# Quarter-wise token blocks and parallel accumulator banks in the prologue of an eight-core hybrid encoder layer

## The chip, the cores and the metric

The kernel runs on one Trainium2 chip, on all 8 of its cores. Each core takes one element of the batch and does the same work as the others. The time is the device time of the slowest core in one execution, in microseconds (us).

In the runs here an execution falls into one of two states. In the slow one, the cores of one die (cores 0 to 3 or 4 to 7) show a lower granted clock of TensorE (undisturbed cores have about 0.99), and the time is longer. Only fast executions are compared here. Where the profiled execution of a kernel was slow on one die, only the cores of the other die are read.

## The reference, cut to what matters

One layer projects the input `x` (2048 prompt tokens and 64 sample tokens per core, 2048 channels) onto the inputs of three branches, and merges the branches. The part that matters here is the first branch, a causal attention with 12 heads of 128 channels, whose logits get a bias from cumulated forget logits:

```python
z = einsum('btd,dn->btn', x, w_in)
q, k, v, f, g_fox, ... = split(z)
logf = log_sigmoid(f + fox_bf)                  # one number per token and head
...
cum = transpose(cumsum(logf, axis=1))           # (B, H, S)
s = einsum('bqhd,bkhd->bhqk', q, k) * scale
s = s + cum[..., queries, None] - cum[..., None, keys]
p = softmax(where(causal, s, NEG_INF))
o = einsum('bhqk,bkhd->bqhd', p, v)             # later multiplied by silu(g_fox)
```

Every head needs four projections of `x`: K, Q, V and the gate G, with 128 weight columns each. The forget logits F of all 12 heads are one projection with only 12 columns.

## The kernel before

The 2112 tokens of a core are cut into five blocks x0 to x4, of 424 or 420 tokens. A projection of one block is 16 matmuls, one for each chunk of 128 channels, which add up in one accumulator bank. The prologue makes the projections of head 0. After it, the attention of head 0 starts, with the projections of head 1 mixed in, so that TensorE always has work. Three more names are needed: *cqb* is the cumulated forget logits of a block of queries, written to DRAM and read back to all partitions. *ncc* is the negative of the same numbers for the keys, laid out by transposes on TensorE. The value transposes (`vtrans`) turn V into the layout that attention needs.

All `x` blocks and weights are loaded through one queue that GpSimd fills, in this order. `load_next(0)` to `load_next(3)` bring the weights of K, Q, V and G of head 0, `load_next(4)` those of K of head 1:

```python
load_x(0, 0)                 # first quarter of x0: 4 of 16 chunks
load_next(0)                 # K weights, 0.5 MB
load_x(0, 1)
load_x(0, 2)
load_x(0, 3)
S.add(POOL, DMA(wf[:], I["w_f"]), writes=[r_wf], dmasem=d_wf)     # F weights
load_next(1)                 # Q weights
load_next(2)                 # V weights
load_x(1)                    # whole block, 1.7 MB
load_next(3)                 # G weights
load_x(2)
load_x(3)
load_x(4)
load_cache(0)
for i in range(4, NSLOT):
    load_next(i)
```

The projections run one after another, each to its end:

```python
for tb in range(5):
    if tb == 0:
        runall(g_k(0, 0)); runall(g_f(0))       # printed on two lines in the kernel
    else:
        runall(g_f(tb)); runall(g_k(0, tb))
    runall(g_q(0, tb))
    runall(g_v(0, tb))
    if tb < 3:
        runall(g_g(0, tb))
    if tb == 3:
        for _ in range(2):
            next_cqb()
ncc_group()                  # 25 transposes
for g in range(5):
    runall(vtrans(0, g))     # 17 transposes
next_cqb()
```

In the profile, every matmul and weight load of a projection has the line L148. The tiles tell them apart: `xT_15` to `xT_19` are x0 to x4, `wf` holds the F weights, `ring_20` K, `ring_21` Q, `ring_22` V and `ring_23` G of head 0, and `ring_24` K of head 1. A second number after a name is a buffer number.

The softmax here doesn't subtract the row's maximum and nothing guards it: scores larger than these inputs give would overflow.

Of the kernel before, what the change touches and what calls it, by code (L numbers as in the profile page):

```python
# [8 lines left out]
F32 = mybir.dt.float32  # L9
# [146 lines left out]
def DMA(out, in_, **kw):  # L156
    return lambda e: e.dma_start(out=out, in_=in_, **kw)  # L157
# [29 lines left out]
NS = 64  # L187
# [165 lines left out]
def build():  # L353
# [35 lines left out]
    sconvT = C0.tile("sconvT", [128, 12, 2], F32, [r_c2])  # L389
    r_ncc = Res("ncc")  # L390
    ncc = C0.tile("ncc", [128, 25, H], F32, [r_ncc])
    r_ut = Res("utail")
# [5 lines left out]
    for b, (t0, n) in enumerate(TB):  # L398
        rs = [Res(f"xT{b}_{i}") for i in range(4)]
        xT.append(SB.at(off, f"xT{b}", [128, 16, n], BF16, rs))  # L400
        r_xT.append(rs)
        d_xT.append([S.dmasem(f"xT{b}_{i}") for i in range(4)] if b == 0 else [S.dmasem(f"xT{b}")] * 4)
        off += 32 * n
# [129 lines left out]

    def g_k(h, tb):
        i = h % 2
        def drain(bk, rb, t0, n):
            t, r = kv32.next()
            S.add(ACT, COPY(t[:, 0:n], bk[:, 0:n]), reads=[rb], writes=[r])
            def f():
                S.add(SP, DMA(O["kT_o"][h, :, t0:t0 + n], t[:, 0:n]), reads=[r], dmasem=d_kv[id(r)])  # L540
                S.add(POOL, COPY(kT[i][:, t0:t0 + n], t[:, 0:n]), reads=[r], writes=[r_k[i][tb]])
            E.later(0.7, f)
        return proj(("K", h), tb, drain, tb == 4)

    def g_v(h, tb):
        def drain(bk, rb, t0, n):
# [5 lines left out]
            E.later(0.7, f)  # L552
        return proj(("V", h), tb, drain, tb == 4)

    def g_q(h, tb):
        i = h % 2
        def drain(bk, rb, t0, n):
            S.add(ACT, COPY(qT[i][:, t0:t0 + n], bk[:, 0:n]), reads=[rb], writes=[r_q[i][tb]])
        return proj(("Q", h), tb, drain, tb == 4)

    def g_g(h, tb):
        def drain(bk, rb, t0, n):
            silu(bk, rb, n, sg[tb][:, 0:n], r_sg[tb], True)
        return proj(("G", h), tb, drain, tb == 4)

# [39 lines left out]

    def load_x(b, q=None):
        if q is None:
            S.add(POOL, DMA(xT[b][:], I[f"xT{b}"]), writes=r_xT[b], dmasem=d_xT[b][0])
        else:
            S.add(POOL, DMA(xT[b][:, 4 * q:4 * q + 4, :], I[f"xT{b}"][:, 4 * q:4 * q + 4, :]),  # L610
                  writes=[r_xT[b][q]], dmasem=d_xT[b][q])
    load_x(0, 0)
    load_next(0)
    load_x(0, 1)
    load_x(0, 2)
    load_x(0, 3)
    S.add(POOL, DMA(wf[:], I["w_f"]), writes=[r_wf], dmasem=d_wf)
    load_next(1)
    load_next(2)
    load_x(1)  # L620
    load_next(3)
    load_x(2)
    load_x(3)
    load_x(4)
    load_cache(0)
    for i in range(4, NSLOT):
        load_next(i)
# [15 lines left out]

    def g_f(tb):
        t0, n = TB[tb]
        bk, rb = PJ.next()
        for k in range(16):
            yield E.pe(MM(bk[0:H, 0:n], wf[:, k, :], xT[tb][:, k, 0:n], k == 0, k == 15), n, [r_wf, r_xT[tb][k // 4]], [rb])
        t, r = et.next()
# [12 lines left out]

    def ncc_group():
        bk, rb = PJ.next()
        for c in range(16):
            E.pe(TR(bk[:, c * H:(c + 1) * H], cumP[:, c * 128:(c + 1) * 128], identf[0:H, 0:H]), 96, [r_cum, r_const], [rb])
        for c in range(9):
            n = 128 if c < 8 else NS
            E.pe(TR(bk[0:n, (16 + c) * H:(17 + c) * H], cumS[:, c * 128:c * 128 + n], identf[0:H, 0:H]), 96, [r_cus, r_const], [rb])
        S.add(DVE, TS(ncc[:, 0:24, :], bk[:, 0:24 * H].rearrange("p (a b) -> p a b", b=H), -1.0, ALU.mult),  # L670
              reads=[rb], writes=[r_ncc])
        S.add(DVE, TS(ncc[0:NS, 24, :], bk[0:NS, 24 * H:25 * H], -1.0, ALU.mult), reads=[rb], writes=[r_ncc])

# [83 lines left out]
    def step(s):  # L757
# [16 lines left out]
        if kc == "A":  # L774
            kcT, rk, _, vc, rv, _ = cache[i]
            y, ry = rl.next()
            def pre():
                S.add(DVE, TT(y[:, :].rearrange("p (c q) -> p c q", q=NS),
                              cq[:, 0:NS].unsqueeze(1).broadcast_to([128, 8, NS]),
                              ncc[:, 16:24, h].unsqueeze(2).broadcast_to([128, 8, NS]), ALU.add),  # L780
                      reads=[rcq, r_ncc], writes=[ry])
            pre()
# [23 lines left out]
        S.add(DVE, STT(x[0:kn, n0:n], sb[0:kn, n0:n], SCALE, cq[0:kn, n0:n], ALU.mult, ALU.add), reads=[rs, rcq], writes=[rx])  # L806
        E.later(T_EXP, lambda: S.add(ACT, ACTF(p[0:kn, n0:n], x[0:kn, n0:n], AF.Exp, bias=bias), reads=[rx, r_ncc], writes=[rp]))
        def facc():
# [84 lines left out]

    for tb in range(5):
        if tb == 0:
            runall(g_k(0, 0))
            runall(g_f(0))
        else:
            runall(g_f(tb))
            runall(g_k(0, tb))  # L900
        runall(g_q(0, tb))
        runall(g_v(0, tb))
        if tb < 3:
            runall(g_g(0, tb))
        if tb == 3:
            for _ in range(2):
                next_cqb()
    ncc_group()
    for g in range(5):
        runall(vtrans(0, g))  # L910
    next_cqb()


# [457 lines left out]
```

## Time and profile before

| before | |
|---|---|
| time, first three executions | median 3448.35 us (3447.11 to 3532.04) |
| TensorE busy, on the profile's page | 97% of the span |
| chain of waits that ended last | 93% TensorE |
| start of block 1, mean of cores 0 to 3 | 48.63 us |
| start of attention (load of its first weights), the same cores | 104.41 us |
| 1600th weight load of the core, counted from 0 (inside head 0's attention) | 309.08 us |

The last rows come from the trace. All kernels here load the same 18,761 sets of weights into TensorE on each core, so the n-th load marks about the same point of the work in each of them. The 1600th lies well past the prologue and everything that moved across its end.

The profiled execution of the kernel before had one die in the slow state. This is the view by cores (span and mean granted clock):

```profile
die 0 (median of its cores): 3439.7 us, clock 0.990
die 1 (median of its cores): 3610.0 us, clock 0.936
```

The second die shows clock 0.936 and is left aside. All readings below are of cores 0 to 3, core 0 if not said otherwise.

The page of the profile is that of the slowest core, here one of the slow die, so only its shares are read. It gives the busy time of each engine, and the first line of the chain that ended last:

```profile
PE 3502.0 (97%) x18761; PEld 1845.2 (51%) x18761; DVE 1202.3 (33%) x2092; ACT 1021.2 (28%) x1846; POOL 771.3 (21%) x962
...
PE 93%; DMA 3%; SPq 1%; ACT 1%; issue 1%; DVE 1%; POOL 1%; POOLq 0%; DVEq 0%; ACTq 0%
```

The kernel is bound by TensorE nearly everywhere. A change of the prologue can only win time in which TensorE stands still or runs at half rate there. The timeline of TensorE on core 0 shows where that is. Its columns are start, duration, engine, line, operation, what is written and read, shape, count, and in brackets the idle time before the group and what ended it:

```profile
13.03 1.57 PE L148 MATMUL bank<-xT_15_57,ring_20_62 128*128 128x424 bf16 x4 [13.03 <-DMA ring_20_62<-w_in]
...
43.45 5.60 PE L148 MATMUL bank<-xT_15_57,ring_23_65 128*128 128x424 bf16 x16 [10.56 <-DMA ring_23_65<-w_in]
48.98 3.03 PE L148 MATMUL bank<-xT_16_58,wf_104 128*12 128x424 bf16 x16
51.95 3.04 PE L148 MATMUL bank<-xT_16_58,ring_20_62 128*128 128x424 bf16 x16
54.82 3.03 PE L148 MATMUL bank<-xT_16_58,ring_21_63 128*128 128x424 bf16 x16
...
101.29 1.15 PE L151 MATMUL bank<-identf_44,cumP_107 12*128 12x12 f32 x16
...
102.90 0.62 PE L154 MATMUL bank<-identb_43,vT_73 128*128 128x128 bf16 x8
103.95 0.89 PE L154 MATMUL bank<-identb_43,vT_73 128*128 128x128 bf16 x9 [0.43 <-DVE ncc_54 L179]
```

The reader is to see four things. The first matmul waits 13 us for the first weights. TensorE then stands 10.56 us until the weights of G land. G itself takes 5.60 us, where a projection takes 3.03 otherwise. From there to the end of block 4 no wait appears at all (the lines left out are all of the kind of those shown, without a bracket). At the end stand the ncc transposes (L151), then the value transposes (L154), with one wait of 0.43 us.

The slow G fits the granted clock in the trace: full from 24.8 us, half from 35.1 to 48.7 us, then full for 949 us. TensorE had stood since 32.9 us, so the clock fell 2.2 us into the wait, and it came back 5.3 us after G's first matmul. On these four cores the half-clock stretch is 10.2 or 13.7 us long, and G's matmuls start 0.35 us apart in place of 0.18. What sets the length of the stretch is not shown.

### The profile page before, as it was taken

How to read it: one execution, taken by the hardware profiler on the slowest of the kernel's cores; microseconds unless marked ns; L12 is line 12 of the kernel's file. 1: busy time of each engine (PE TensorE's matmuls, PEld its weight loads, DVE VectorE, ACT ScalarE, POOL GpSimd, SP SyncE). 2: the span in 40 equal slices, each digit the busy share in tenths (PEclk: the TensorE clock that was granted, in tenths of full speed). 3: DMA queues.
4: the chain of work that ended last, by engine and by line, in shares of the span. 5: the costliest groups of instructions: out<-in, count | busy, mean ns of one | idle time of the engine just before them, and what ended most of it. 6: DMA issues, size and time to landing. Idle time of an engine off the chain costs nothing.

```text
span 3614.3 us, 54781 instructions; the slowest of 8 cores (3434.6 to 3614.3 us)
## 1 busy us (share of the span) xinstructions
PE 3502.0 (97%) x18761; PEld 1845.2 (51%) x18761; DVE 1202.3 (33%) x2092; ACT 1021.2 (28%) x1846; POOL 771.3 (21%) x962
## 2 busy tenths in 40 slices
PE   6999999999999989999999999999999999999898
PEld 3444444544444545555555554555555555555343
DVE  1455555555556722222222221111111111111365
ACT  1455555555555410010104552111111111111111
POOL 1222222222222211111111221000022223332133
PEclk8888888888888999999999999999999999999999
DMA  9423333333222243333323216333455545655743
GB/s 167 97 64 70 70 70 68 66 67 66 66 63 66 46 69 65 68 62 56 61 50 59 47 38 164 90 98 85 116 143 133 138 118 131 141 125 136 206 173 117
DMA packets 183608, 337.45 MB, mean 93 GB/s; under 512 B 31204, under 2 KB 135388, under 8 KB 177000
## 3 DMA queue, kind: packets, MB, share of 16 engines
q0 software_dynamic: 39744, 134.55, 22.9%
q1 hardware_dynamic: 143592, 199.39, 17.9%
q8 instruction: 156, 2.56, 0.3%
q14 instruction: 116, 0.95, 0.1%
HBM read 362.26 MB, written 106.13 MB: 130 GB/s over the span
## 4 chain that ended last, share of the span: by engine, by line
PE 93%; DMA 3%; SPq 1%; ACT 1%; issue 1%; DVE 1%; POOL 1%; POOLq 0%; DVEq 0%; ACTq 0%
PE bank L148 93%; DMA ring_23_65<-w_in 1%; SPq L157 1%; DMA a_scr_3<-ao_59_101 1%; PE bank L154 0%; DMA memT_134<-memT 0%; DMA mb_scr<-gt_114_156 0%; DMA x_147_189<-xp 0%; DMA a_4_112_154<-a_scr_4 0%; ACT rl_83_125 L165 0%; DVE on_85_127 L175 0%; ACT pt_71_113 L165 0%; POOL ao_59_101 L175 0%; DVE acc_78_120 L175 0%; ACT qT_74 L170 0%
## 5 line engine op out<-in xcount | busy, mean ns | idle before, releaser
L175 DVE TENSOR_TENSOR mt_115_157<-bank,gt_113_155 128x424 f32<-128x424 f32 (+1 forms) x120 | 71.8, 598 | 517.8 <-PE bank L148 448.5
L175 DVE TENSOR_TENSOR mt_116_158<-bank,gt_114_156 128x424 f32<-128x424 f32 (+1 forms) x120 | 71.8, 598 | 494.1 <-PE bank L148 463.9
L165 ACT ACTIVATE gt_113_155<-bank,bm_50 128x424 f32<-128x424 f32 (+1 forms) x120 | 73.6, 613 | 506.3 <-PE bank L148 455.6
L165 ACT ACTIVATE gt_114_156<-bank,bm_50 128x424 f32<-128x424 f32 (+1 forms) x120 | 73.6, 613 | 499.4 <-PE bank L148 470.8
L148 PE MATMUL bank<-xT_15_57,ring_20_62 128*128 128x424 bf16 x400 | 84.5, 359 | 17.9 <-DMA ring_20_62<-w_in 13.9
L148 PE MATMUL bank<-qT_70,kT_71 128*128 128x512 bf16 (+4 forms) x246 | 96.2, 391 | 0.0
L148 PE MATMUL bank<-qT_74,kT_75 128*128 128x512 bf16 (+4 forms) x246 | 94.5, 384 | 0.2 <-DVE st_69_111 L183 0.2
L148 PE MATMUL bank<-xT_17_59,ring_26_68 128*128 128x424 bf16 x416 | 86.2, 352 | 4.8 <-ACT qT_74 L170 4.8
L148 PE MATMUL bank<-xT_17_59,ring_22_64 128*128 128x424 bf16 x416 | 86.8, 354 | 4.0 <-ACT qT_70 L170 4.0
L148 PE MATMUL bank<-xT_16_58,ring_24_66 128*128 128x424 bf16 x432 | 90.2, 353 | 0.0
L148 PE MATMUL bank<-xT_19_61,ring_24_66 128*128 128x420 bf16 x432 | 89.4, 351 | 0.0
L148 PE MATMUL bank<-xT_15_57,ring_24_66 128*128 128x424 bf16 x432 | 89.2, 356 | 0.0
L148 PE MATMUL bank<-xT_17_59,ring_24_66 128*128 128x424 bf16 x432 | 88.7, 353 | 0.0
L148 PE MATMUL bank<-xT_18_60,ring_24_66 128*128 128x420 bf16 x432 | 88.2, 351 | 0.0
L148 PE MATMUL bank<-xT_16_58,ring_26_68 128*128 128x424 bf16 x416 | 87.7, 354 | 0.0
L148 PE MATMUL bank<-xT_16_58,ring_22_64 128*128 128x424 bf16 x416 | 87.2, 354 | 0.0
L148 PE MATMUL bank<-xT_15_57,ring_26_68 128*128 128x424 bf16 x416 | 86.6, 354 | 0.0
L148 PE MATMUL bank<-xT_15_57,ring_22_64 128*128 128x424 bf16 x416 | 86.2, 354 | 0.0
L148 PE MATMUL bank<-xT_19_61,ring_22_64 128*128 128x420 bf16 x416 | 84.9, 351 | 0.3
L148 PE MATMUL bank<-xT_18_60,ring_22_64 128*128 128x420 bf16 x416 | 85.1, 351 | 0.0
L148 PE MATMUL bank<-xT_19_61,ring_26_68 128*128 128x420 bf16 x416 | 84.5, 349 | 0.4 <-ACT qT_74 L170 0.2
L148 PE MATMUL bank<-xT_18_60,ring_26_68 128*128 128x420 bf16 x416 | 84.5, 349 | 0.0
(917 smaller groups left out, 7352.2 us busy)
## 6 DMA issues: line engine op xcount, KB each, us to landing
ring_24_66<-w_in POOLq DMA_DIRECT2D x15, 512.0 KB, 6.7
ring_21_63<-w_in POOLq DMA_DIRECT2D x14, 512.0 KB, 8.0
ring_22_64<-w_in POOLq DMA_DIRECT2D x14, 512.0 KB, 7.8
ring_23_65<-w_in POOLq DMA_DIRECT2D x14, 512.0 KB, 6.8
ring_25_67<-w_in POOLq DMA_DIRECT2D x14, 512.0 KB, 8.2
ring_26_68<-w_in POOLq DMA_DIRECT2D x14, 512.0 KB, 6.7
ring_27_69<-w_in POOLq DMA_DIRECT2D x14, 512.0 KB, 6.6
ring_20_62<-w_in POOLq DMA_DIRECT2D x13, 512.0 KB, 7.1
```

Of the source, the lines that this page charges most:

```text
L148: return lambda e: e.matmul(out, lhsT=lhsT, rhs=rhs, start=start, stop=stop)
L157: return lambda e: e.dma_start(out=out, in_=in_, **kw)
L165: return lambda e: e.activation(out=out, in_=in_, func=func, **kw)
L175: return lambda e: e.tensor_tensor(out=out, in0=in0, in1=in1, op=op)
```

## The change

The change is meant to make TensorE wait less for data in the prologue. Each of x1 to x4 is loaded in four quarters of 4 chunks, as x0 was. The projections of a block, F, K, V, Q and G, are run quarter by quarter, each in an accumulator bank of its own. So all matmuls that a quarter allows can run before the next quarter lands. Besides that, four things move: the G weights are now loaded before x1; the F weights come after the V weights; block 0 computes F after V; and the first 8 ncc transposes and 12 of the 17 value transposes are put between blocks 3 and 4, while the other ncc transposes run 5 us into attention.

The diff, cut to its core:

```diff
-        d_xT.append([S.dmasem(f"xT{b}_{i}") for i in range(4)] if b == 0 else [S.dmasem(f"xT{b}")] * 4)
+        d_xT.append([S.dmasem(f"xT{b}_{i}") for i in range(4)])
...
-    S.add(POOL, DMA(wf[:], I["w_f"]), writes=[r_wf], dmasem=d_wf)
     load_next(1)
     load_next(2)
-    load_x(1)
+    S.add(POOL, DMA(wf[:], I["w_f"]), writes=[r_wf], dmasem=d_wf)
     load_next(3)
-    load_x(2)
-    load_x(3)
-    load_x(4)
+    for b in range(1, 5):
+        load_x(b)                     # now four quarters each
+    load_next(4)
     load_cache(0)
-    for i in range(4, NSLOT):
+    for i in range(5, NSLOT):
         load_next(i)
...
+    PPJ = Ring(BK)
+    def pro_block(tb, gens):
+        t0, n = TB[tb]
+        bs = [PPJ.next() for _ in gens]
+        for q in range(4):
+            for (key, drain), (bk, rb) in zip(gens, bs):
+                for k in range(4 * q, 4 * q + 4):
+                    ...               # one matmul of this projection, chunk k
+                if q == 3:
+                    ...
+                    drain(bk, rb, t0, n)
...
-    for tb in range(5):
-        ...                           # F, K, Q, V, G one after another
-    ncc_group()
-    for g in range(5):
+    runall(g_k(0, 0))
+    runall(g_q(0, 0))
+    runall(g_v(0, 0))
+    pro_block(0, [(None, d_f(0))])
+    runall(g_g(0, 0))
+    for tb in range(1, 5):
+        gens = [(None, d_f(tb)), (("K", 0), g_k(0, tb, True)), (("V", 0), g_v(0, tb, True)), (("Q", 0), g_q(0, tb, True))]
         if tb < 3:
-            runall(g_g(0, tb))
+            gens.append((("G", 0), g_g(0, tb, True)))
+        pro_block(tb, gens)
         if tb == 3:
-            for _ in range(2):
-                next_cqb()
+            next_cqb()
+            next_cqb()
+            ncc_group(0)
+            for g in range(3):
+                runall(vtrans(0, g))
+    for g in range(3, 5):
         runall(vtrans(0, g))
     next_cqb()
+    E.later(5.0, lambda: ncc_group(1))
```

More of the change, by code (lines that the diff above doesn't have):

```diff
@@ L389, in build @@
     sconvT = C0.tile("sconvT", [128, 12, 2], F32, [r_c2])
-    r_ncc = Res("ncc")
-    ncc = C0.tile("ncc", [128, 25, H], F32, [r_ncc])
+    r_ncc, r_ncc2 = Res("ncc"), Res("ncc2")
+    ncc = C0.tile("ncc", [128, 25, H], F32, [r_ncc, r_ncc2])
     r_ut = Res("utail")
@@ L531, in silu, with g_k @@
         E.later(0.9, s1)
-    def g_k(h, tb):
+    def g_k(h, tb, raw=False):
         i = h % 2
@@ L542, in drain, with g_v @@
             E.later(0.7, f)
-        return proj(("K", h), tb, drain, tb == 4)
-    def g_v(h, tb):
+        return drain if raw else proj(("K", h), tb, drain, tb == 4)
+    def g_v(h, tb, raw=False):
         def drain(bk, rb, t0, n):
@@ L552, in drain, with g_q @@
             E.later(0.7, f)
-        return proj(("V", h), tb, drain, tb == 4)
-    def g_q(h, tb):
+        return drain if raw else proj(("V", h), tb, drain, tb == 4)
+    def g_q(h, tb, raw=False):
         i = h % 2
@@ L558, in drain, with g_g @@
             S.add(ACT, COPY(qT[i][:, t0:t0 + n], bk[:, 0:n]), reads=[rb], writes=[r_q[i][tb]])
-        return proj(("Q", h), tb, drain, tb == 4)
-    def g_g(h, tb):
+        return drain if raw else proj(("Q", h), tb, drain, tb == 4)
+    def g_g(h, tb, raw=False):
         def drain(bk, rb, t0, n):
             silu(bk, rb, n, sg[tb][:, 0:n], r_sg[tb], True)
-        return proj(("G", h), tb, drain, tb == 4)
+        return drain if raw else proj(("G", h), tb, drain, tb == 4)
     def blks(t0, n):
@@ L604, in build, with load_x @@
     et = Ring(ctr.items)
-    def load_x(b, q=None):
-        if q is None:
-            S.add(POOL, DMA(xT[b][:], I[f"xT{b}"]), writes=r_xT[b], dmasem=d_xT[b][0])
-        else:
+    def load_x(b):
+        for q in range(4):
             S.add(POOL, DMA(xT[b][:, 4 * q:4 * q + 4, :], I[f"xT{b}"][:, 4 * q:4 * q + 4, :]),
                   writes=[r_xT[b][q]], dmasem=d_xT[b][q])
-    load_x(0, 0)
-    load_next(0)
-    load_x(0, 1)
-    load_x(0, 2)
-    load_x(0, 3)
-    S.add(POOL, DMA(wf[:], I["w_f"]), writes=[r_wf], dmasem=d_wf)
+    for q in range(4):
+        S.add(POOL, DMA(xT[0][:, 4 * q:4 * q + 4, :], I["xT0"][:, 4 * q:4 * q + 4, :]), writes=[r_xT[0][q]], dmasem=d_xT[0][q])
+        if q == 0:
+            load_next(0)
     load_next(1)
     load_next(2)
-    load_x(1)
+    S.add(POOL, DMA(wf[:], I["w_f"]), writes=[r_wf], dmasem=d_wf)
     load_next(3)
-    load_x(2)
-    load_x(3)
-    load_x(4)
+    for b in range(1, 5):
+        load_x(b)
+    load_next(4)
     load_cache(0)
-    for i in range(4, NSLOT):
+    for i in range(5, NSLOT):
         load_next(i)
@@ L642, in build, with d_f, drain_f @@
     d_cs = [S.dmasem(f"cs{b}") for b in range(6)]
-    def g_f(tb):
+    PPJ = Ring(BK)
+    def pro_block(tb, gens):
         t0, n = TB[tb]
-        bk, rb = PJ.next()
-        for k in range(16):
-            yield E.pe(MM(bk[0:H, 0:n], wf[:, k, :], xT[tb][:, k, 0:n], k == 0, k == 15), n, [r_wf, r_xT[tb][k // 4]], [rb])
+        bs = [PPJ.next() for _ in gens]
+        for q in range(4):
+            for (key, drain), (bk, rb) in zip(gens, bs):
+                for k in range(4 * q, 4 * q + 4):
+                    if key is None:
+                        E.pe(MM(bk[0:H, 0:n], wf[:, k, :], xT[tb][:, k, 0:n], k == 0, k == 15), n, [r_wf, r_xT[tb][q]], [rb])
+                    else:
+                        w, rw = W(key)
+                        E.pe(MM(bk[:, 0:n], w[:, k, :], xT[tb][:, k, 0:n], k == 0, k == 15), n, [rw, r_xT[tb][q]], [rb])
+                if q == 3:
+                    if key is not None and tb == 4:
+                        Wfree(key)
+                    drain(bk, rb, t0, n)
+    def d_f(tb):
+        return lambda bk, rb, t0, n: drain_f(tb, bk, rb, t0, n)
+    def drain_f(tb, bk, rb, t0, n):
         t, r = et.next()
@@ L661, in g_f, with ncc_group @@
             S.add(SP, DMA(cum_scr[:, NP:NP + NS], cumS[:, PAST:PAST + NS]), reads=[r_cus], writes=[r_cscr[5]], dmasem=d_cs[5])
-    def ncc_group():
+    def ncc_group(part):
         bk, rb = PJ.next()
-        for c in range(16):
+        if part == 0:
+            for c in range(8):
+                E.pe(TR(bk[:, c * H:(c + 1) * H], cumP[:, c * 128:(c + 1) * 128], identf[0:H, 0:H]), 96, [r_cum, r_const], [rb])
+            S.add(DVE, TS(ncc[:, 0:8, :], bk[:, 0:8 * H].rearrange("p (a b) -> p a b", b=H), -1.0, ALU.mult),
+                  reads=[rb], writes=[r_ncc])
+            return
+        for c in range(8, 16):
             E.pe(TR(bk[:, c * H:(c + 1) * H], cumP[:, c * 128:(c + 1) * 128], identf[0:H, 0:H]), 96, [r_cum, r_const], [rb])
@@ L669, in ncc_group @@
             E.pe(TR(bk[0:n, (16 + c) * H:(17 + c) * H], cumS[:, c * 128:c * 128 + n], identf[0:H, 0:H]), 96, [r_cus, r_const], [rb])
-        S.add(DVE, TS(ncc[:, 0:24, :], bk[:, 0:24 * H].rearrange("p (a b) -> p a b", b=H), -1.0, ALU.mult),
-              reads=[rb], writes=[r_ncc])
-        S.add(DVE, TS(ncc[0:NS, 24, :], bk[0:NS, 24 * H:25 * H], -1.0, ALU.mult), reads=[rb], writes=[r_ncc])
+        S.add(DVE, TS(ncc[:, 8:24, :], bk[:, 8 * H:24 * H].rearrange("p (a b) -> p a b", b=H), -1.0, ALU.mult),
+              reads=[rb], writes=[r_ncc2])
+        S.add(DVE, TS(ncc[0:NS, 24, :], bk[0:NS, 24 * H:25 * H], -1.0, ALU.mult), reads=[rb], writes=[r_ncc2])
     SRING = Ring(BK[3:5])
@@ L780, in pre @@
                               ncc[:, 16:24, h].unsqueeze(2).broadcast_to([128, 8, NS]), ALU.add),
-                      reads=[rcq, r_ncc], writes=[ry])
+                      reads=[rcq, r_ncc2], writes=[ry])
             pre()
@@ L806, in step @@
         S.add(DVE, STT(x[0:kn, n0:n], sb[0:kn, n0:n], SCALE, cq[0:kn, n0:n], ALU.mult, ALU.add), reads=[rs, rcq], writes=[rx])
-        E.later(T_EXP, lambda: S.add(ACT, ACTF(p[0:kn, n0:n], x[0:kn, n0:n], AF.Exp, bias=bias), reads=[rx, r_ncc], writes=[rp]))
+        E.later(T_EXP, lambda: S.add(ACT, ACTF(p[0:kn, n0:n], x[0:kn, n0:n], AF.Exp, bias=bias),
+                                   reads=[rx, r_ncc if kc != "B" and kc < 8 else r_ncc2], writes=[rp]))
         def facc():
@@ L891, in conv_groups @@
                 yield from proj((nm, c), tb, d, tb == 4)
-    for tb in range(5):
-        if tb == 0:
-            runall(g_k(0, 0))
-            runall(g_f(0))
-        else:
-            runall(g_f(tb))
-            runall(g_k(0, tb))
-        runall(g_q(0, tb))
-        runall(g_v(0, tb))
+    runall(g_k(0, 0))
[5 more added lines that the diff above has]
+        gens = [(None, d_f(tb)), (("K", 0), g_k(0, tb, True)), (("V", 0), g_v(0, tb, True)), (("Q", 0), g_q(0, tb, True))]
         if tb < 3:
-            runall(g_g(0, tb))
+            gens.append((("G", 0), g_g(0, tb, True)))
+        pro_block(tb, gens)
         if tb == 3:
-            for _ in range(2):
-                next_cqb()
-    ncc_group()
-    for g in range(5):
+            next_cqb()
[4 more added lines that the diff above has]
+    for g in range(3, 5):
         runall(vtrans(0, g))
     next_cqb()
+    E.later(5.0, lambda: ncc_group(1))
     st = A0.ring("st", 3, [128, 512], F32)
```

## The prediction

> Durations are from the profiled run before the change, on the undisturbed die (cores 0 to 3, clock 0.99; the other die was in the slow state).
>
> **What bounds it now.** The page gives TensorE 97% of the span; the chain that ended last is 93% TensorE. By stretches, TensorE is busy about 19 of every 20 us except in the first 60. So only idle or half-rate time in the prologue can be won. In the timeline of core 0 (core 1 in brackets), TensorE
> - starts at 13.0 us (12.9), when the first weights land;
> - waits 4.0 us (3.3) between the quarters of the first x block;
> - finishes the first K at 23.3 (22.5), then F, Q, V;
> - idles 10.6 us (8.9) until the G weights land at 43.4 (42.2). Loads land in issue order: x1 at 39.7, these weights, x2 at 53.6, x3 at 63.8, x4 at 76.6;
> - runs G cold: 5.5 us against 2.95 warm. [...] (matmul spacing 0.35 against 0.18 us);
> - from 49.0 to attention at 104.7 never waits on a load: x2 is used 10 us after landing, x3 14 us.
>
> So quarters and parallel banks attack a wait that blocks 1 to 4 do not have. What helps is a side effect: the G weights are queued before x1.
>
> **Costing.** By landing times, 0.5 MB of weights take 3.3 us, an x block 10.5.
> - First K unchanged, done at 23.3.
> - Q's weights land at about 25.1, and F no longer fills the gap: new wait 1.8 us, then cold for some 3 us (1.5 to 2 lost, as F lost before).
> - V, F follow at once. G reuses F's bank and waits for F's Exp: 0.75 us.
> - G weights land near 32 us, before use: the 10.6 us wait and 2.5 us of cold G are gone.
> - Block 1 starts near 39 instead of 49.0. The last x1 quarter lands near 43, needed near 50; later blocks have more slack.
> - New handover waits: ncc transposes come 2.15 us after F, but Exp, Ln, negation and scan take 3.1: 1 us after block 3. Value transposes after block 4 wait 1.2 us for V's two copies, queued behind F and K. Before, one 0.43 us wait. Net loss 1.8.
> - Half of ncc moves into attention; same work.
> - 12 more load issues of 0.5 us on GpSimd: the queue is backed up far beyond that; worth 0.
>
> Sum: core 0 10.0 - 1.8 = 8.2 us; core 1 about 7; core 2 about 8.3. All on the critical path: TensorE bounds everything after, and later weights land well ahead.
>
> **Prediction.** 3440 us in the fast state (0.24% less); 8 in 10 between 3433 and 3447. Faster by over 2%: 0.01; within 2%: 0.98; slower: 0.01.
>
> **What would show it.** Right: no wait on G's weights; Q waits 1 to 3 us on its own; block 1 begins at 38 to 41 us; no TensorE wait on quarters of x1 to x4; attention starts near 96 to 97; waits of about 1 us before the first ncc transposes and the last value transposes; then a constant shift. Wrong: waits on x quarters, attention at 104 or later, or the shift lost in the first head.
>
> **What would make it wrong.** Quarter transfers moving fewer bytes per us than whole blocks; half clock lasting longer after the gappy start; the first head meeting the tail of loads (last at 95 us); or noise: two fast runs before differ by 1.2 us, but a slow one is 2.4% longer (3532).

That Q would be "cold for some 3 us" is an estimate from the profile of before, where F of block 0 took 3.77, 4.98, 4.81 and 5.22 us on cores 0 to 3, in place of 3.03.

## The result, and the profile after

| | before | after |
|---|---|---|
| median of 4 executions | 3447.73 us | 3442.94 us |
| fast executions | 3448.35, 3447.11, 3446.31 | 3442.97, 3442.92, 3441.89 |
| the slow one | 3532.04 | 3510.87 |
| ratio after to before, fast runs | | 0.9986, 95% interval 0.9964 to 1.0009 |

A ratio here is the mean time of one kernel's fast runs over the mean time of the other's fast runs of the same rounds, so it is not quite the ratio of the medians quoted beside it. A ratio between 0.98 and 1.02 counts as the same time. A second set of runs on another chip (*after_again* below) gave 0.9986 once more, with the interval 0.9973 to 0.9998.

The change is worth 4.8 us by the medians, 0.14% (4.7 us by the means of the fast executions; each median also counts the slow one). The first interval alone does not exclude that there is no gain; the second one does, narrowly. The predicted 3440 lies 2.9 us below the measured median and its range holds it. But the range is 14 us wide, wider than the gain that was promised, 8.2 us. So the time alone says little about the reasoning, and the mechanism has to be looked at term by term.

The profiled execution after was fast on both dies:

```profile
die 0 (median of its cores): 3433.1 us, clock 0.992
die 1 (median of its cores): 3435.6 us, clock 0.991
```

The page of its slowest core shows the same kind of kernel as before:

```profile
PE 3319.1 (96%) x18642; PEld 1787.8 (52%) x18761; DVE 1220.9 (35%) x2093; ACT 1015.1 (29%) x1846; POOL 783.6 (23%) x974
...
PE 92%; DMA 3%; issue 1%; ACT 1%; DVE 1%; SPq 1%; POOL 1%; POOLq 0%; ACTq 0%; DVEq 0%
```

The timeline of TensorE on core 0, in the same columns:

```profile
25.11 5.00 PE L148 MATMUL bank<-xT_15_57,ring_21_63 128*128 128x424 bf16 x16 [2.12 <-DMA ring_21_63<-w_in]
...
36.84 3.03 PE L148 MATMUL bank<-xT_15_57,ring_23_65 128*128 128x424 bf16 x16 [0.90 <-ACT ct_55_97 L165]
39.80 0.88 PE L148 MATMUL bank<-xT_16_58,wf_104 128*12 128x424 bf16 x4
40.61 0.89 PE L148 MATMUL bank<-xT_16_58,ring_20_62 128*128 128x424 bf16 x4
41.34 0.88 PE L148 MATMUL bank<-xT_16_58,ring_22_64 128*128 128x424 bf16 x4
42.06 0.88 PE L148 MATMUL bank<-xT_16_58,ring_21_63 128*128 128x424 bf16 x4
42.77 0.88 PE L148 MATMUL bank<-xT_16_58,ring_23_65 128*128 128x424 bf16 x4
43.59 0.88 PE L148 MATMUL bank<-xT_16_58,wf_104 128*12 128x424 bf16 x4
...
83.67 0.63 PE L151 MATMUL bank<-identf_44,cumP_107 12*128 12x12 f32 x8 [1.30 <-DVE cumP_107 L634]
...
85.20 0.88 PE L148 MATMUL bank<-xT_19_61,wf_104 128*12 128x420 bf16 x4
...
98.25 0.22 PE L154 MATMUL bank<-identb_43,vT_73 128*128 128x128 bf16 x1 [0.76 <-ACT qT_70 L170]
98.88 0.50 PE L154 MATMUL bank<-identb_43,vT_73 128*128 128x128 bf16 x4 [0.41 <-POOL vT_73 L171]
...
104.53 0.66 PE L151 MATMUL bank<-identf_44,cumP_107 12*128 12x12 f32 x8
```

The reader is to see, against the timeline of before: the long wait for `ring_23` and the slow G are gone, and block 1 begins at 39.80 us in place of 48.98. In their place stand a wait of 2.12 us for Q's weights with a slow Q of 5.00 us after it, and 0.90 us before G. From block 1 on, the groups are of 4 matmuls. A group of `wf` is followed by the next after 0.81 us (39.80 to 40.61), and the group ahead of `wf` after 0.82 us (42.77 to 43.59), while the groups among themselves are 0.71 to 0.73 us apart. And there are three new waits, 1.30 us before the first ncc transposes and 0.76 and 0.41 us at the last value transposes, where there was one of 0.43. The last row is the beginning of the second part of the ncc transposes, now inside attention.

The milestones, in us from the start of the span, as means over undisturbed cores (before: cores 0 to 3; of *e2_order* and *e3_order_quarters* the six cores whose clock did not fall; otherwise all eight; attention is the load of its first weights, and head 1's first K projection, which the texts often name in its place, starts 0.2 to 0.5 us later):

| kernel | block 1 | block 2 | block 3 | block 4 | attention | 1600th load |
|---|---|---|---|---|---|---|
| before | 48.63 | 63.16 | 77.70 | 89.31 | 104.41 | 309.08 |
| after | 39.86 | 55.00 | 70.14 | 85.26 | 99.37 | 305.06 |
| after_again | 39.91 | 55.05 | 70.19 | 85.31 | 99.42 | 305.10 |
| e1_f_alone | 40.17 | 55.75 | 70.28 | 83.46 | 96.48 | 302.16 |
| e2_order | 43.07 | 59.99 | 74.52 | 86.14 | 101.24 | 306.20 |
| e3_order_quarters | 35.87 | 58.11 | 72.64 | 84.26 | 99.45 | 305.78 |
| e4_old_order | 48.18 | 63.32 | 78.46 | 93.58 | 107.69 | 313.37 |
| e5_k_first | 43.04 | 59.94 | 74.47 | 86.09 | 101.19 | 306.25 |
| e7_whole_loads | 43.00 | 59.49 | 74.63 | 89.76 | 104.69 | 310.36 |
| e8_combined | 35.08 | 49.89 | 64.15 | 78.21 | 90.44 | 303.82 |
| e9_early_cqb | 34.92 | 49.76 | 64.03 | 78.53 | 93.67 | 299.12 |

On the way from block 1 to the 1600th load, the lead of the change over before shrinks from 8.8 us to 4.0. It is 8.2 us at block 2, 7.6 at block 3, 4.1 at block 4 and 5.0 at attention. (The jump between block 3 and block 4 is in part bookkeeping: 1.5 us of transposes were moved there from the end of the prologue. For the same reason the 5.0 at attention overstates the lead by 1.1 us, the ncc transposes that are still to come.)

### The profile page after: what moved, and what is told of

Read it like the earlier page. It is cut to its first block, busy times and chain, and to the rows that moved or that the text cites. A ratio compares the mean times of both kernels' runs of the same rounds, so it can differ in the third digit from the quotient of the medians.

```text
span 3441.4 us, 54705 instructions; the slowest of 8 cores (3427.9 to 3441.4 us)
## 1 busy us (share of the span) xinstructions
PE 3319.1 (96%) x18642; PEld 1787.8 (52%) x18761; DVE 1220.9 (35%) x2093; ACT 1015.1 (29%) x1846; POOL 783.6 (23%) x974
## 3 DMA queue, kind: packets, MB, share of 16 engines
q1 hardware_dynamic: 143592, 199.39, 19.5%
## 4 chain that ended last, share of the span: by engine, by line
PE 92%; DMA 3%; issue 1%; ACT 1%; DVE 1%; SPq 1%; POOL 1%; POOLq 0%; ACTq 0%; DVEq 0%
PE bank L148 91%; SPq L157 1%; DMA ring_21_63<-w_in 1%; DMA a_scr_3<-ao_59_101 1%; DMA memT_134<-memT 0%; DMA mb_scr<-gt_114_156 0%; DMA x_147_189<-xp 0%; PE bank L154 0%; DMA a_4_112_154<-a_scr_4 0%; DVE st_69_111 L183 0%; POOL hl_82_124 L175 0%; DVE on_85_127 L175 0%; ACT rl_84_126 L165 0%; ACT qT_74 L170 0%; POOL hl_80_122 L175 0%
## 5 line engine op out<-in xcount | busy, mean ns | idle before, releaser
L148 PE MATMUL bank<-xT_15_57,ring_20_62 128*128 128x424 bf16 x400 | 81.6, 351 | 17.0 <-DMA ring_20_62<-w_in 12.4
L148 PE MATMUL bank<-xT_17_59,ring_26_68 128*128 128x424 bf16 x416 | 82.7, 342 | 6.0 <-ACT qT_74 L170 6.0
L148 PE MATMUL bank<-xT_17_59,ring_21_63 128*128 128x424 bf16 x416 | 83.3, 342 | 5.0 <-ACT qT_70 L170 5.0
L148 PE MATMUL bank<-xT_15_57,ring_21_63 128*128 128x424 bf16 x416 | 85.3, 351 | 2.9 <-DMA ring_21_63<-w_in 2.9
L148 PE MATMUL bank<-xT_16_58,ring_24_66 128*128 128x424 bf16 x432 | 86.1, 342 | 0.1
L148 PE MATMUL bank<-xT_19_61,ring_24_66 128*128 128x420 bf16 x432 | 85.4, 340 | 0.3
L148 PE MATMUL bank<-xT_17_59,ring_24_66 128*128 128x424 bf16 x432 | 84.8, 342 | 0.0
L148 PE MATMUL bank<-xT_15_57,ring_24_66 128*128 128x424 bf16 x432 | 84.4, 342 | 0.0
L148 PE MATMUL bank<-xT_18_60,ring_24_66 128*128 128x420 bf16 x432 | 84.4, 340 | 0.0
L148 PE MATMUL bank<-xT_16_58,ring_26_68 128*128 128x424 bf16 x416 | 83.7, 342 | 0.3
L148 PE MATMUL bank<-xT_16_58,ring_21_63 128*128 128x424 bf16 x416 | 83.7, 342 | 0.3
L148 PE MATMUL bank<-xT_15_57,ring_26_68 128*128 128x424 bf16 x416 | 82.5, 342 | 0.0
L148 PE MATMUL bank<-xT_19_61,ring_21_63 128*128 128x420 bf16 x416 | 81.7, 340 | 0.8 <-ACT qT_70 L170 0.3
L148 PE MATMUL bank<-xT_19_61,ring_26_68 128*128 128x420 bf16 x416 | 81.3, 340 | 0.9 <-ACT qT_74 L170 0.3
L148 PE MATMUL bank<-xT_18_60,ring_21_63 128*128 128x420 bf16 x416 | 81.9, 340 | 0.3
L148 PE MATMUL bank<-xT_18_60,ring_26_68 128*128 128x420 bf16 x416 | 81.4, 340 | 0.3
L148 PE MATMUL bank<-xT_16_58,ring_20_62 128*128 128x424 bf16 x400 | 80.3, 343 | 0.1
L148 PE MATMUL bank<-xT_19_61,ring_20_62 128*128 128x420 bf16 x400 | 79.7, 340 | 0.3
```

The lines of the kernel that those rows point to most:

```text
L148: return lambda e: e.matmul(out, lhsT=lhsT, rhs=rhs, start=start, stop=stop)
```

## The experiments

Theory 1, formed from the timelines above: what is lost from block to block is the interleaving of F. Whenever TensorE goes from a projection with 128 weight columns to F with 12, or back, the next matmul starts 0.096 us later than usual (275 ns after the one before, in place of 179). Before, a block had 2 such switches. After, it has 8. The rival is that changing the accumulator bank after every 4 matmuls is what costs, whichever projections alternate. Theory 2: nearly all of the gain is the G weights' place in the load queue, and the quarters are worth little by themselves.

The runs were made in three batches, each on one chip, with runs of the kernel before beside them (medians 3445.87, 3447.96 and 3446.32 us with the slow runs counted, 3445.22, 3446.80 and 3445.65 us of the fast runs alone).

### e1_f_alone: F in one piece

The change, but F of each block runs its 16 matmuls in one piece ahead of the others, which stay interleaved:

```diff
     for tb in range(1, 5):
-        gens = [(None, d_f(tb)), (("K", 0), ...), (("V", 0), ...), (("Q", 0), ...)]
+        pro_block(tb, [(None, d_f(tb))])
+        gens = [(("K", 0), ...), (("V", 0), ...), (("Q", 0), ...)]
```

> The change, but in blocks 1 to 4 the forget projection F (12 weight columns) runs in one piece ahead of the quarter loop; K, V, Q, G stay interleaved by quarters. After the change a block of five projections took 15.14 us instead of 14.54. Theory 1 (each switch between 128-column and 12-column weights costs about 0.09 us, and there are 8 a block instead of 2): block 2 takes 14.5 to 14.6 us, K, V, Q, G still 0.72 us per quarter, the 1.30 us wait before the ncc transposes is gone because F's chain starts earlier, up to 1 us is lost on the last quarters of x1; head 1's first K projection starts near 96.5 to 97.0 us (mean of cores) against 99.7; total about 3440. Rival (alternating between PSUM banks every four matmuls costs it): block 2 stays above 15.0 us and that start is 98 or later.

Measured: median 3437.31 us, ratio to before 0.9977 (0.9960 to 0.9995). The timeline of TensorE, core 0:

```profile
43.16 0.88 PE L148 MATMUL bank<-xT,wf 128*12 128x424 bf16 x4 [0.59 <-DMA xT<-xT]
...
55.54 3.03 PE L148 MATMUL bank<-xT,wf 128*12 128x424 bf16 x16
...
70.08 3.02 PE L148 MATMUL bank<-xT,wf 128*12 128x420 bf16 x16
73.03 8.73 PE L148 MATMUL bank<-xT,ring 128*128 128x420 bf16 x48
81.69 0.66 PE L151 MATMUL bank<-identf,cumP 12*128 12x12 f32 x8
```

Block 2 takes 14.54 us from its F to the F of block 3 (55.54 to 70.08), as long as in the kernel before, though K, V, Q and G still change banks after every 4 matmuls. The rival is refuted and theory 1 holds. The wait before the ncc transposes is gone as well: F ends 8.7 us ahead of them, so its logarithm and scan are done. The price is in the first line: F of block 1 has to wait 0.59 us for the last quarter of x1, since nothing else may run in between. At the 1600th load this kernel is 2.9 us ahead of the change.

### e2_order: only the G weights' place

The kernel before, with one line moved:

```diff
-    load_x(1)
     load_next(3)
+    load_x(1)
```

> The kernel before, with one line moved: the G weights are queued ahead of x block 1, which is still one load. Theory (the queue order is what pays): no wait on the G weights, G of block 0 done near 36 us; but x1 lands whole only near 43 us, so TensorE waits about 7 us for it and the next projection runs cold; block 1 starts near 43.5 us, effective gain 4 us; head 1's first K projection near 101 us (before: 104.9); total about 3444. Rival (the quarters do nothing even with the new order): no wait on x1 and that start at 96 us or earlier.

Measured: median 3469.75 us; the fast runs 3467.2, 3468.49, 3469.75; ratio 1.0070 (1.0051 to 1.0088). This was a clear miss, and not for a reason that either theory had. On six of the eight cores the prologue went as foreseen: attention began at 101.24 us and the spans were 3432 to 3441 us. On the other two, TensorE's granted clock fell to 0.81. These are rows of the view by stretches (the stretch, its length, busy time and count of each engine, then granted clock, DMA share and GB/s), first for core 6:

```profile
54.00:130.00 76.00, 75.65 (x377) 37.66 (x376) 17.11 (x32) 25.39 (x49) 11.13 (x19) 0.81 0.79 143
...
214.00:600.00 386.00, 374.53 (x2235) 202.18 (x2233) 269.39 (x464) 237.92 (x443) 117.32 (x172) 1.00 0.43 83
```

and for core 5 in the same execution:

```profile
54.00:130.00 76.00, 75.55 (x464) 40.74 (x462) 25.96 (x48) 31.73 (x61) 15.38 (x27) 1.00 0.90 165
```

Core 6 does 377 matmuls between 54 and 130 us, where core 5 does 464. By the records of the clock, core 6 fell at 53.5 us, 5.9 us after it had come back to full clock, and core 7 at 53.3 us, 7.2 us after. Both stayed at 0.81 for 160.9 us and then returned to full clock, with the load unchanged. Every fast run of e2_order in this batch has one or more such pairs of cores, with spans near 3459 to 3468 us. So the slowest core is some 25 us late, and the gain of the order is buried under it. What it is worth without a fall is read from the undisturbed cores: 2.9 us at the 1600th load.

### e3_order_quarters: the order and the quarters, projections one after another

e2_order, with x1 to x4 loaded in quarters, and the sequential projections of before:

```diff
-    load_x(2)
-    load_x(3)
-    load_x(4)
+    for q in range(4):
+        load_x(1, q)
+    ...                               # the same for x2, x3, x4
```

> As e2, and x1 to x4 are loaded in quarters with a semaphore each; the projections stay one after the other. Theory: F of block 1 starts near 36 us and waits for each quarter (landing about 34, 37, 40, 43), done near 44 instead of 46 to 47 in e2; no new handover waits; head 1's first K projection near 97.5 to 98.5 us; total about 3440, so equal to or faster than the full change. Rival (parallel banks carry the gain): that start is later than the 99.7 us of the change.

Measured: median 3464.89 us, ratio 1.0053 (1.0035 to 1.0071), with the same falls of pairs of cores. On the undisturbed cores attention begins at 99.45 us, a little later than expected. The waits of TensorE in block 1, core 0:

```profile
38.18 0.88 PE L148 MATMUL bank<-xT,wf 128*12 128x424 bf16 x4 [0.72 <-DMA xT<-xT]
...
40.68 0.88 PE L148 MATMUL bank<-xT,wf 128*12 128x424 bf16 x4 [1.62 <-DMA xT<-xT]
...
43.62 1.57 PE L148 MATMUL bank<-xT,wf 128*12 128x424 bf16 x4 [2.06 <-DMA xT<-xT]
```

Without parallel banks, F is first and needs all four quarters at once, so TensorE stands in front of each. F begins 7.2 us earlier than in e2_order, and only 1.9 us of this are left at block 2. At the 1600th load 0.4 us are left, as all six undisturbed cores drop to half clock for 3.4 us at the start of attention, where only one of the six in e2_order does. At the start of attention this kernel is level with the change (99.45 against 99.37 us), where the theory had it ahead and the rival behind. So quarters alone are worth at most 1.9 us: there must be other work to do on each quarter.

### e4_old_order: the change without the G weights' new place

```diff
     S.add(POOL, DMA(wf[:], I["w_f"]), writes=[r_wf], dmasem=d_wf)
+    load_x(1)
     load_next(3)
-    for b in range(1, 5):
+    for b in range(2, 5):
         load_x(b)
```

> The change, but the G weights are again queued behind x block 1. Theory: quarters and parallel banks alone win nothing: TensorE waits about 7 us for the G weights near 36 to 43 us, G runs cold, block 1 starts near 48 to 49 us, head 1's first K projection near 108 to 109 us (before 104.9, change 99.7); total about 3450 to 3452. Rival (quarters and banks carry the gain): that start at 102 us or earlier.

Measured: median 3450.40 us, ratio 1.0014 (0.9993 to 1.0036); attention at 107.69 us, as expected. The wait for the weights of G is back (core 0):

```profile
44.01 4.80 PE L148 MATMUL bank<-xT,ring 128*128 128x424 bf16 x16 [7.26 <-DMA ring<-w_in]
```

Blocks 1 and 2 are as long as in the change (15.14 us each), so all that the interleaving and the new handovers cost is still paid, and nothing is gained for it. At the 1600th load this kernel is 4.3 us behind the one before. The order is what the gain rests on.

### e7_whole_loads: the change with whole blocks

```diff
     def load_x(b):
-        for q in range(4):
-            S.add(POOL, DMA(xT[b][:, 4 * q:4 * q + 4, :], I[f"xT{b}"][:, 4 * q:4 * q + 4, :]),
-                  writes=[r_xT[b][q]], dmasem=d_xT[b][q])
+        S.add(POOL, DMA(xT[b][:], I[f"xT{b}"]), writes=r_xT[b], dmasem=d_xT[b][0])
```

> The change with x1 to x4 again as one load each, all else kept. Theory: block 1 is ready at 39.9 us and x1 lands whole near 42.8, so its start moves to about 43 us, perhaps with a few us at half clock; blocks 2 to 4 land in time; first attention matmul near 102.5 to 104 us (mean of cores; change 99.4, before 104.4); so the quarters are worth 3 to 5 us, and only in block 1. Rival (my prediction's step that quarters are worth nothing): 99.4 to 100 us.

Measured: only one fast run, 3448.85 us, so the time itself gives no interval. Attention begins at 104.69 us, a little later than expected and later than before. Block 1 waits for the whole of x1 (core 0):

```profile
41.78 0.88 PE L148 MATMUL bank<-xT,wf 128*12 128x424 bf16 x4 [1.87 <-DMA xT<-xT]
```

Block 1 starts 3.1 us later than in the change, seven of the eight cores drop to half clock for 3.4 to 6.8 us, six of them in block 1, and the 1600th load is 5.3 us later. So the change as it is written needs the quarters: without them, its whole gain is gone. Theory 2 is half right. With the projections one after another, the order alone keeps 2.9 of the change's 4.0 us at the 1600th load (e2_order), and quarters add little to it. With interleaved projections, which also have F's switches and the new handover waits to pay for, the quarters decide. With the old order nobody waited for x1. With the new order x1 lands about 3 us later and is wanted earlier, and then parallel work on quarters is what hides it.

The kernels can be put side by side, at the 1600th load: order alone 306.20, order and quarters 305.78, order and parallel banks without quarters 310.36, all three 305.06, and with F taken out of the interleaving 302.16, against 309.08 before. (They are not clean corners: the last three also have the change's moved transposes.) So quarters and banks, on top of the order, are worth 1.1 us as the change has them, and 4.0 us with F in one piece.

### after_again: the change on another chip

> The change itself, unaltered, once more beside the others on this chip: total 3441 to 3443, ratio to before 0.9985 to 0.999, first attention matmul near 99.4 us.

Measured: median 3443.32 us, ratio 0.9986 (0.9973 to 0.9998), with all milestones within 0.05 us of the first profile. The result stands.

### e5_k_first, e2_again and e5_again: the falls of the clock

e5_k_first is e2_order with K ahead of F in block 1:

```diff
+        elif tb == 1:
+            runall(g_k(0, tb))
+            runall(g_f(tb))
```

> As e2 (old kernel, G weights ahead of x1, one load per x block), but in block 1 K runs before F. In all fast runs of e2 one or two pairs of cores fell to 0.81 of the clock for 160.8 us, 5 to 7 us after their second return to full clock, and cost 25 us; the kernel before had none. Theory A (in e2 the weak 12-column F runs at half clock, so the return to full clock goes straight into 11.6 us of dense 128-column matmuls, while in the kernel before F fills the first 3 us at full clock): with K at half clock and F after it, no pair falls to 0.81 in fast runs, total near 3441 to 3443. Theory B (the wait for x1 near 36 to 43 us brings it on by itself): pairs still fall, total 3460 to 3470.

Measured: one fast run, 3444.6 us, and four slow ones. No pair of cores on an undisturbed die fell. The batch was on another chip, so the two kernels were run again side by side on a third.

> e2 unaltered, because e2 and e5 ran on two chips. If the fall to 0.81 belongs to the program: in every fast run one to three pairs of cores at a mean clock of 0.982 and some 25 us longer, total 3462 to 3470. If it belonged to the other chip: none, total near 3442.

> e5 (e2 with K before F in block 1) unaltered, on the same chip as e2 now. If the order of F and K after the wait decides: no pair at 0.982 in fast runs and on undisturbed dies of slow runs, total 3442 to 3446. If chance or the chip decided: pairs fall as in e2.

Measured: e2_again had fast runs of 3440.24 and 3440.59 us without a fall and one of 3469.32 us with two pairs fallen (ratio 1.0027, 0.9983 to 1.0070). e5_again had fast runs of 3442.51 and 3442.13 us (ratio 0.9990, 0.9971 to 1.0009). Counted in pairs of cores on undisturbed dies, e2_order fell in 8 of 16 on the first chip and in 2 of 14 on the third, and e3_order_quarters in 5 of 16 on the first. e5_k_first fell in 0 of 12 on the second and 0 of 16 on the third. The kernel before fell in 0 of 100.

That every fast run of e2 would fall was wrong: on the third chip one of three did. Whether the chip makes the difference, or chance, is not shown. On the same chip, 2 of 14 against 0 of 16 does not decide whether F directly after the return to full clock is the trigger. This stays open. What is shown is that such falls exist, that they cost 25 us, and that without them one moved line makes a kernel of 3440 us, 5.5 us below the mean of the fast runs of before in that batch (3445.88 us). From two executions, that is about what the whole change gains (4.7 us, on another chip), though at the 1600th load the change keeps 1.1 us more.

Is the slow state something else? The profile of the kernel before, whose die 1 was slow, speaks against it. Between 240 and 300 us, core 4 of that die is at 0.81 and core 6 is not:

```profile
240.00:300.00 60.00, 58.28 (x286) 28.73 (x284) 31.03 (x52) 27.97 (x50) 12.83 (x21) 0.81 0.29 66
...
240.00:300.00 60.00, 57.37 (x344) 31.09 (x348) 43.93 (x78) 39.43 (x76) 19.34 (x28) 1.00 0.40 78
```

By the records of the clock, cores 4 and 5 fell to 0.81 at 30.8 and 31.0 us, 4.4 and 4.5 us after they had come to full clock, and cores 6 and 7 only at 2547 us. One of the stretches at 0.81 of cores 4 and 5 lasted 161.3 us. So here too the clock falls to 0.81 by pairs of cores, only more often and for longer, and the kernel before has such falls as well. The 0 of 100 is counted on dies that were not slow. A whole die at a mean clock of 0.81 does occur in slow runs (e7_whole_loads, 4104.03 us: 0.810 to 0.813 on cores 0 to 3). That the falls and the slow state are the same thing is likely, but not shown.

### e8_combined: everything that the runs had suggested

The change's loads, with the F weights moved up to just behind the K weights and F of block 0 interleaved with K, so that the wait for x0's quarters and for Q's weights is filled; F of blocks 1 and 2 in one piece behind the others, F of blocks 3 and 4 ahead of them; V first; one ring of banks for all:

```diff
         if q == 0:
             load_next(0)
+            S.add(POOL, DMA(wf[:], I["w_f"]), writes=[r_wf], dmasem=d_wf)
...
+    pro_block(0, [(("K", 0), g_k(0, 0, True)), (None, d_f(0))])
...                                          # Q, V, G of block 0
     for tb in range(1, 5):
+        gens = [V, K, Q]                     # abridged
         if tb < 3:
             gens.append(G)
+        else:
+            pro_block(tb, [(None, d_f(tb))])
         pro_block(tb, gens)
+        if tb < 3:
+            pro_block(tb, [(None, d_f(tb))])
```

> A version built from what was found: the change's order of loads and quarters, w_f ahead of the second x0 quarter and F of block 0 interleaved with K of block 0 (its matmuls fill the waits for x0); F of blocks 1 and 2 after the quarter loop, F of blocks 3 and 4 before it (no switching inside, its chain done before the ncc transposes); V first in the loop, so its copies are done before the value transposes; all prologue projections from one ring of banks, so G no longer waits for F's bank. Expected: block 1 starts near 34 to 36 us (change 39.9), first attention matmul near 90 to 92 us (change 99.4, F alone 96.5), no waits before ncc and value transposes, no core below full clock after its ramp, total 3430 to 3434, so 12 to 15 us below the kernel before. If it is not below 3436, the accounting by waits and switches is wrong.

Measured: median 3442.19 us, ratio 0.9981 (0.9969 to 0.9993). Another miss. The prologue was what had been expected, with attention at 90.44 us, 9 us ahead of the change. But then the lead shrank to 1.2 us at the 1600th load. The waits between 88 and 110 us on core 0 (who waited for whom: us in total, times, longest), taken from the longer list:

```profile
DVE st L183 <- DMA lf_o<-logfT: 14.8, 1, 14.8
...
PE bank L148 <- DVE st L183: 6.0, 1, 6.0
```

TensorE stands 6.0 us for VectorE, which makes the first attention step (`st`), and VectorE had waited for a DMA, the write of the last forget logits from `logfT` to the output. The tile `st` is laid over the memory of `logfT`, so it may not be written before that write has read it:

```python
P0 = Region(SB, PRO, SB_HI)              # prologue only, begins at PRO: wf, then logfT, ...
...                                      # A0.top is PRO at the end of the prologue
st = A0.ring("st", 3, [128, 512], F32)   # the first tiles of attention, at the same place
```

That write is 20 KB. It was issued at 83.8 us and is done at 99.85 us on core 0, and it is the releaser on all eight cores (96.9 to 99.9 us). It was issued after the two cqb broadcasts of 256 KB each, by the same engine, as the timeline of SyncE on core 0 shows:

```profile
78.00 1.31 SPq L157 DMA_DIRECT2D cqb<-cum_scr  x2
83.83 0.33 SPq L157 DMA_DIRECT2D lf_o<-logfT  x1
```

The broadcasts were issued at 78.0 and 78.7 us and land at 94.6 and 99.2 us; on every core the write is done with the second broadcast or up to 1.4 us after it. The first broadcast, which the first attention step reads, lands at 92.6 to 94.6 us, after attention has begun. So a faster write alone would not have ended the wait before that. The view by stretches shows what all three met, first for e8_combined, core 0 (the number before the last is the mean busy share of the core's 16 DMA engines):

```profile
95.00:101.00 6.00, 0.21 (x2) 0.18 (x3) 1.05 (x2) 0.21 (x1) 0.00 (x0) 0.89 1.06 187
```

and for the change, core 0:

```profile
95.00:101.00 6.00, 4.82 (x29) 2.42 (x28) 2.44 (x4) 3.35 (x7) 3.16 (x5) 1.00 0.32 55
```

Between 95 and 101 us the DMA engines are full in e8_combined (1.06), while in the change the loads come to a pause (0.32), and the write of the last forget logits, issued at 97.1 us, holds nothing up there. In e8_combined the weights of later heads are loaded earlier too, since buffers come free earlier (issued from 91.6 us on, in place of 98.7, on core 0), and the last load of the prologue lands at 102.6 us in place of 93.8, so there is no such pause. Even in the change, though, the two broadcasts took 11.5 us each on core 0. Nor did they wait in e8_combined for the whole backlog of loads: on core 0 they landed at 94.6 and 99.2 us, ahead of the last load of the prologue, which had been issued before them (GpSimd issues no load between 60 and 91.6 us) and landed at 102.6. How the DMA engines divide their time between the queues is not shown. In this run the first broadcast took 16.6 us and the second 19.5, as medians over the cores. All cores then also drop to half clock for 3.4 to 10.2 us.

### e9_early_cqb: the broadcasts after block 2

e8_combined, with the two broadcasts issued one block earlier:

```diff
-        if tb == 3:
+        if tb == 2:
             next_cqb()
             next_cqb()
+        if tb == 3:
             ncc_group(0)
```

> e8 with the first two broadcasts of the cumulated forget logits (what the first attention steps on VectorE wait for) requested after block 2 instead of after block 3. In e8 the prologue ended 9 us earlier than in the change, at 90.4 us, but TensorE then stood 4 to 6 us and fell to half clock, because VectorE waited until about 100 us for this load, in a DMA queue full without a break until about 106 us. Theory (only the landing of that load was late): first attention matmul again near 90.5 us, matmul number 1600 near 295 to 296 us (before 309, change 305, e8 304), no half clock near 100 us, total 3431 to 3435. Rival (the DMA queue as a whole is now the bound): the wait moves to another load, number 1600 at 300 us or later, total 3438 or more.

(The text on record names the broadcast as what VectorE waited for. The trace names the write behind it, as shown above.)

Measured: median 3436.47 us; fast runs 3434.85, 3435.67, 3436.47 and 3434.21; ratio 0.9969 (0.9955 to 0.9984). It is the fastest kernel of its batch: its fast runs have a mean of 3435.3 us, those of before 3445.9. The change did not run on that chip, and the intervals of the two ratios to before overlap; the lead over the change is read at the 1600th load, 5.9 us. The wait of VectorE is gone on seven of eight cores (the eighth is still released by the same write, at 95.5 us). Attention begins at 93.67 us, though, and not at the expected 90.5, mostly because a new wait comes inside block 4, where F wants the last quarter of x4 (core 0):

```profile
83.09 0.88 PE L148 MATMUL bank<-xT,wf 128*12 128x420 bf16 x4 [1.85 <-DMA xT<-xT]
```

The last quarter of x4 now lands at about 83 us, where the whole of x4 had landed at 76 us in the change. On core 1 the wait is 3.57 us, and two cores drop to half clock with it. The rival for this run, that the DMA queue as a whole is the next bound, is right in part. The experiment moved the broadcasts and, through the queue, the write behind them together; it does not tell which of the two would have been enough.

### e1_again: the simplest mend, on a third chip

> F alone ahead of the quarter loop, unaltered, beside the combined version on this chip: total 3436 to 3439, ratio to before about 0.9977, first attention matmul near 96.5 us.

Measured: median 3438.47 us, ratio 0.9977 (0.9964 to 0.9990), the same as on the first chip. One moved projection gives the change another 3 us or so: 7.9 us less than before in ratio (0.0023 times 3446), against 4.8.

## Why the prediction was right, and where it was wrong

The time, 3440 us with a range of 3433 to 3447, held: 3442.94 was measured. The size of the gain was overstated, 8.2 us predicted and 4.8 measured. By terms, on core 0:

| term of the sum | predicted | measured on core 0 |
|---|---|---|
| block 1 starts earlier (wait for G weights and cold G gone; less new waits for Q and G's bank) | 10.0 us | 9.18 (48.98 to 39.80) |
| interleaved F | not in the sum | -2.26 |
| waits at ncc and value transposes | -1.8 | -2.50 |
| half of ncc moved into attention | 0 | 0 |
| sum | 8.2 | 4.42 |
| 1600th load earlier | | 4.42 (309.43 to 305.01) |

The term of F is the growth of the four blocks, 0.61, 0.61, 0.52 and 0.52 us. The term of the transposes is counted from start to start. It is 1.45 us between the end of block 3's matmuls and the first transpose, 0.90 and 0.55 us at the last value transposes, less 0.40 for the one wait of before. As idle times the profile shows 1.30, 0.76 and 0.41, less 0.43.

1. *"TensorE bounds everything after"* and only the prologue can be won: right. From the 1600th load to the end, the two kernels take 3129.9 and 3129.4 us (mean spans 3438.97 and 3434.41, less 309.08 and 305.06). In the other kernels this rest takes 3127.1 to 3130.7 us, so from one execution each a lead of 1 or 2 us at the 1600th load does not yet prove a gain in time.
2. *"What helps is a side effect: the G weights are queued before x1"*: right, and e4_old_order shows it. Without it the change is 4.3 us slower than before at the 1600th load.
3. *"Q's weights land at about 25.1, and F no longer fills the gap: new wait 1.8 us"*: right. The wait is 2.12 us and Q is slow (5.00 us).
4. *"Block 1 starts near 39"*: right, 39.86 us in the mean.
5. *"No TensorE wait on quarters of x1 to x4"*: right for the change.
6. *"So quarters and parallel banks attack a wait that blocks 1 to 4 do not have"*: true of the kernel before and wrong as a judgement of what they are worth. The new order makes that wait: e2_order and e3_order_quarters have it, and e7_whole_loads loses the whole gain with it. The prediction's own sum used the quarters, when it let block 1 start at 39 us with the last quarter of x1 landing at 43. As for the weight of the two, its judgement stands for a sequential prologue: the order alone is worth 2.9 of the 4.0 us.
7. *"Waits of about 1 us before the first ncc transposes and the last value transposes ... Net loss 1.8"*: right in kind, 0.7 us too small.
8. *"12 more load issues ... worth 0"*: right; none of the five waits of TensorE between 22 and 110 us on core 0 (0.4 to 2.1 us) is for an issue.
9. *"Attention starts near 96 to 97"*: wrong, 99.37. This is the step that failed. The sum silently took the matmuls of a block to be worth the same in any order, so blocks of the same length as before. The runs showed that each switch between 12 and 128 weight columns costs 0.096 us, and the change has 24 more of them: 24 times 0.096 is 2.3 us. e1_f_alone takes the switches away and gets the time back.

The missed term could have been read from the kernel before: in its timeline a projection with `wf` is followed by the next after 2.97 us (48.98 to 51.95), while K is followed by Q after 2.87. That was overlooked. The traces show that going from weights of 128 columns to weights of 12, or back, costs 0.096 us each time. What makes the 0.096 us stays open.

## What to carry to other kernels

When work is interleaved more finely, count the switches between unlike matmuls (here of 12 and 128 weight columns) and read the cost of one from the trace of the kernel before: a 0.1 us step that was paid twice per block can be paid eight times. Ask of every load order which wait it removes and which it creates, since here the reordering made the wait that the quarters and banks then hid. Test the smallest part of a change by itself, too: one moved line gained about as much as the whole change where the clock did not fall, and without that line the rest of the change is 4.3 us behind the old kernel at the 1600th load (e4_old_order). And when a stage is made earlier, look at what its small transfers will now collide with: 9 us won in the prologue were mostly given back at the next handover, until two broadcasts had been moved ahead of the crowd.
